# A different order for the dot products of gathered u rows, and a different pace for their fetches

## The chip, the cores and the metric

The kernel runs on one core of a Trainium2 chip. The metric is the device time of one execution in microseconds (us). Before the change three runs took 3755.72, 3756.43 and 3759.92 us; the median is 3756.43.

The engines are named as in the profile: PE is TensorE (matmuls; PEld are its weight loads), DVE is VectorE, ACT is ScalarE, POOL is GpSimd and SP is SyncE, which issues most of the plain transfers. Each engine works through its own list of instructions in order; an instruction that waits holds up all that stand behind it on its engine.

## The reference

The model is two layers of a mixer (attention, pooling, convolution, gates) with an expert feed-forward, and then two layers of a second block. Only the feed-forward of layer 0 is touched by the change:

```python
def peer_ffn(x, w_q, sub_keys, u_emb, v_emb):          # 512 tokens in layer 0, in chunks of 128
    def chunk(xc):
        q = (xc @ w_q).reshape(PEER_CHUNK, PEER_HEADS, 2, PEER_HALF)
        s = jnp.einsum('thid,hikd->thik', q, sub_keys).astype(jnp.float32)
...
        top_s, pos = lax.top_k(cand, PEER_TOPK)        # 16 experts for each of 8 heads
        eidx = jnp.take_along_axis(cidx, pos, axis=-1)
        gate = jax.nn.softmax(top_s, axis=-1)
        u = u_emb[eidx]
        hid = jax.nn.gelu(jnp.einsum('td,thkd->thk', xc, u))
        wgt = (gate * hid.astype(jnp.float32)).astype(xc.dtype)
        return jnp.einsum('thk,thkd->td', wgt, v_emb[eidx])
```

There are 16384 experts; a row of `u_emb` or `v_emb` has 1024 float32 values. A token picks 8 x 16 = 128 of them.

## The kernel before, in words

**Two ways through the feed-forward.** In layer 0 the last 128 of the 512 tokens (NROW) go the way of the reference: their 128 u rows and 128 v rows per token are gathered from memory by index. This is the class `Rows`. The other 384 tokens go the dense way: all 16384 hidden values are computed with matmuls against the whole of `u`, masked by a gate matrix, and multiplied by the whole of `v`. Each float32 matmul is made of three (high by high, high by low, low by high part), so a weight is split by ACT (`uhi`, `vhi`, L358) and DVE (`ulo`, `vlo`, L359). Layer 1 has 256 tokens, all on the dense way.

**Stages of the dense way in layer 0.** (1) `select` picks the experts. (2) `expand` turns the picks into the gate matrix: for each of 48 groups of 8 tokens DVE makes two one-hot tiles, `ohA` (L1509) and `ohB` (L1511), each from two buffers, PE multiplies them (`ps_g`, L1524 and L1525) and ACT copies the result to `stage` (L1527). Woven into (1) and (2) are the 84 hidden chunks of the first 42 blocks (`lead`, `hidden`): 24 matmuls `ps_mm` of 384 columns each (L390 to L392), then the activation `hs` (L1563). `PAY` sets how many chunks stand beside each step: a step `r` of the routing pays for 2.9 of them, a step `g` of the expansion for 0.8; what is left runs after the last `g`. (3) The value stage runs over 64 blocks in turns of two: blocks whose hidden part is still to be made (22 of them, two chunks each) and blocks whose hidden part is read back from memory (`hs_r<-hd`). A block loads 1 MB of `v` (and 1 MB of `u` if its hidden part is made here), multiplies by the gates G on DVE (L1210), splits into `Wh` and `Wl`, and PE adds it up: four products into the accumulators `keep` and two into `ps_v` (L1266), which DVE adds to `racc` (L1233). `ps_v` and `ps_mm` share three PSUM buffers. Every second block also brings 1 MB of modulation weights (`ps_mod`).

**The row path.** `Rows.ticks` is a generator; `next` on it does one tick. In its first part tick p fetches u row p of all 128 tokens (one indirect DMA on POOL, L258, 128 rows of 4 KB into a `row` tile of five buffers) and forms the dot products of row p - 3 with the tokens on DVE (L272: one custom instruction that writes its products over the row, and one that reads the sum out to `hid`). After 131 ticks the hidden values are finished and the second part does the same with v rows; there the row goes into small matmuls (`ps_row`, L304) four ticks later. It has 131 ticks too.

**When a tick happens.** After each product of PE, the program calls `spend` with the estimated time of that product. It adds the time, multiplied by `rate`, to an account, and does a tick whenever the account holds `pace` microseconds. `rate` is SLOW (0.7) from the start of the expansion until the value stage, where it is 1.0. `pace` is 3.5 in the u part and 3.25 in the v part (PACE).

```python
    def spend(self, us):
        if self.begun:
            self.due += us * self.rate
            while self.due >= self.pace:
                self.due -= self.pace
                next(self.steps, None)
```

The time of n matmuls of width w is `n * (w / 2.3 + 13) / 1000` us: 16 of 64 columns for a group of the expansion, 24 of 384 for a hidden chunk, 6 of 512 for a value product.

**What sets the order.** The program text doesn't fix the order of instructions on an engine. A planner at build time simulates all engines with estimated durations and puts each instruction on its engine's list when, by that simulation, its inputs are there. Two things bind the planner: data (with buffers), and edges written by hand. `fetch` writes one such edge: the fetch waits for `beat`, the last matmul of the last product ahead of it in the program. Its class is Sync, so the engine also waits for it on the chip by a semaphore. The dot product has no edge by hand: it follows its row's DMA and nothing else.

Of the kernel before, what the change touches and what calls it, by code (L numbers as in the profile page):

```python
# [16 lines left out]
ALU = mybir.AluOpType  # L17
# [29 lines left out]
PAY = ((2.9, 0.8), (5.0, 1.2))  # L47
NROW = 128
ROWBUFS = 5
PACE = (3.5, 3.25)  # L50
SLOW = 0.7
NPV = 4


# [154 lines left out]
class Rows:  # L209
# [21 lines left out]
    def begin(self, d1, d2, te):  # L231
# [10 lines left out]
        self.hid = pool.tile([P, P], F32, tag="hid", name="hid")  # L242
        self.steps, self.pace = self.ticks(), PACE[0]

# [11 lines left out]
    def fetch(self, name, idx):  # L256
        row = self.pool.tile([P, D], F32, tag="row", name="row", bufs=ROWBUFS)
        ins = self.nc.gpsimd.indirect_dma_start(row, None, self.p.g[name], bass.IndirectOffsetOnAxis(ap=idx, axis=0))  # L258

        self.p.tc.add_manual_dep(ins.ins, self.p.beat.ins.name, mybir.DependencyInfo(mybir.DependencyClass.Sync, mybir.DependencyReason.DATA),  # L260
                                 reason="pace")
        return row

    def ticks(self):
        nc, pool, prog = self.nc, self.pool, self.p
        rows = {}
        for p in range(P + 3):
            if p < P:
                rows[p] = self.fetch("urow", self.eu[:, p:p + 1])
            if p >= 3:  # L270
                row = rows.pop(p - 3)
                nc.vector.tensor_tensor_reduce(out=row, in0=row, in1=self.xt, op0=ALU.mult, op1=ALU.add, scale=1.0, scalar=0.0,  # L272
                                               accum_out=self.hid[:, p - 3:p - 2])
            yield
        self.pace = PACE[1]
        pt = prog.pm.tile([P, P], F32, tag="mm", name="ps_e")
        nc.tensor.transpose(pt, self.ef, prog.ident)
        self.ev = pool.tile([P, P], U32, tag="ev", name="ev")
        nc.vector.tensor_copy(self.ev, pt)
        nc.scalar.activation(self.hid, self.hid, AF.Gelu_apprx_tanh)  # L280
        nc.vector.tensor_tensor(self.hid, self.hid, self.gate, op=ALU.mult)
        order = [(r, i, g) for r in range(2) for i in range(32) for g in range(2)]
        ps = wt = None
        for n in range(P + 3):
            if n == 2:
                pt = prog.pm.tile([P, P], F32, tag="mm", name="ps_w")
                nc.tensor.transpose(pt, self.hid, prog.ident)
                wt = pool.tile([P, 2, 2, 32], F32, tag="wt", name="wt")
                nc.scalar.activation(wt.rearrange("p r g i -> p (r g i)"), pt, AF.Copy)
            if n < P:  # L290
                r, i, g = order[n]
                t = r * 64 + g * 32 + i
                rows[n] = self.fetch("vrow", self.ev[:, t:t + 1])
            if n >= 4 and n % 2 == 0:
                r, i, _ = order[n - 4]
                m = pool.tile([P, 2, 32], F32, tag="mask", name="mask2", bufs=4)
                nc.vector.tensor_tensor(m, self.hit[:, None, 31 - i:63 - i].to_broadcast([P, 2, 32]),
                                        wt[:, r, :, i:i + 1].to_broadcast([P, 2, 32]), op=ALU.mult)
                if i == 0:
                    ps = self.pv.tile([P, 512], F32, tag="rowv", name="ps_row")  # L300
                for h in range(2):
                    for g in range(2):
                        c = 32 * (2 * h + g)
                        nc.tensor.matmul(ps[c:c + 32, :], m[:, g, :], rows[n - 4 + g][:, h * 512:(h + 1) * 512],  # L304
                                         start=(i == 0), stop=(i == 31), tile_position=(0, c))
                del rows[n - 4], rows[n - 3]
                if i == 31:
                    self.add(r, ps)
            yield
# [17 lines left out]
class Prog:  # L327
# [1164 lines left out]
    def expand(self, l, T, picks, gd):  # L1492

        nc = self.nc
        with self.tc.tile_pool(name=f"expand{l}", bufs=1, reuse_waits="tile") as kp:
# [6 lines left out]
            if self.rows:  # L1502
                self.rows.begun, self.rows.rate = True, SLOW
            for n in range(T // 8 + 1):
# [421 lines left out]
```

## Time and profile before

| | before |
|---|---|
| median of 3 runs | 3756.43 us |
| profiled execution | 3769.55 us, span 3767.8 us |
| PE busy | 3588.1 us (95%) |
| DVE busy | 2460.4 us (65%) |
| ACT busy | 1635.9 us (43%) |
| POOL busy | 604.9 us (16%) |
| DMA | 777.60 MB, mean 206 GB/s |

Busy times are of the profiled execution, whose own time stands beside its span: the span runs from the first to the last instruction of the program. The expansion of layer 0 begins at about 950 us; the first u row is fetched at 976.0 us, the last at 1613.4, the first v row at 1629.3 and the last at 2153.4 us. The expansion of layer 1 ends near 2893 us.

### The profile page before, as it was taken

To read this page: it belongs to the slowest core of one execution; us is meant where nothing else is said; L and a number is where in the kernel's file an instruction comes from. 1 tells how busy PE (TensorE), PEld (TensorE's weight loads), DVE (VectorE), ACT (ScalarE), POOL (GpSimd) and SP (SyncE) were. 2 spreads that over 40 slices of the span, in tenths; PEclk is the share of its full clock that TensorE was granted. 3 is DMA by queue.
4 is the path that set the end of the run, shared out by engine and by line. 5 is a ranking of instruction groups with operands and counts; after the bars stand their busy time and mean duration, and the time that the engine had idled before them with its cause. 6 is when DMAs were issued, how large, how long until landed. Compare 5 with 4: busy or idle time off the path is not lost. (4 is left out here: it accounts for less than half of the span.)

```text
span 3767.8 us, 55009 instructions
## 1 busy us (share of the span) xinstructions
PE 3588.1 (95%) x21681; PEld 3104.3 (82%) x21681; DVE 2460.4 (65%) x4540; ACT 1635.9 (43%) x2608; POOL 604.9 (16%) x686
## 2 busy tenths in 40 slices
PE   7999999899988889899999999999999999999999
PEld 5988877789888777777766699999899888887787
DVE  5566555698687667654445576778977655556675
ACT  3333333346565322222222245455667444445454
POOL 0112222100122222222222221222000000002121
PEclk9999999999999999999999999999999999999999
DMA  5222245225687978788888823344578767666453
GB/s 208 73 90 73 79 162 190 89 90 181 237 300 277 334 268 291 287 302 299 308 287 304 286 95 119 119 153 168 188 260 291 249 238 240 235 227 221 146 177 111
DMA packets 227764, 777.60 MB, mean 206 GB/s; under 512 B 17297, under 2 KB 100753, under 8 KB 168497
## 3 DMA queue, kind: packets, MB, share of 16 engines
q1 hardware_dynamic: 165984, 567.29, 42.9%
q0 software_dynamic: 37184, 135.41, 10.4%
q10 hardware_dynamic: 24336, 71.38, 4.9%
q8 instruction: 170, 2.79, 0.3%
q14 instruction: 90, 0.73, 0.1%
HBM read 705.60 MB, written 68.42 MB: 205 GB/s over the span
## 5 line engine op out<-in xcount | busy, mean ns | idle before, releaser
L358 ACT ACTIVATE uhi<-wraw 128x1024 fp32r<-128x1024 f32 x586 | 609.7, 1057 | 868.0 <-PE ps_mm L391 341.9
L390 PE MATMUL ps_mm<-xh,uhi 128*128 128x256 f32 (+2 forms) x2952 | 960.8, 325 | 19.3 <-DVE racc L1233 9.1
L392 PE MATMUL ps_mm<-xh,ulo 128*128 128x256 f32 (+2 forms) x2952 | 945.8, 321 | 8.7 <-DVE ulo L359 8.7
L391 PE MATMUL ps_mm<-xl,uhi 128*128 128x256 f32 (+2 forms) x2952 | 944.7, 320 | 0.0
L359 DVE TENSOR_TENSOR ulo<-wraw,uhi 128x1024 fp32r<-128x1024 f32 x586 | 718.0, 1237 | 294.9 <-ACT uhi L358 274.4
L390 PEld LDWEIGHTS ps_mm<-xh,uhi 128*128 128x128 f32 x2952 | 566.2, 192 | 64.1 <-DVE racc L1233 15.8
L392 PEld LDWEIGHTS ps_mm<-xh,ulo 128*128 128x128 f32 x2952 | 565.9, 192 | 31.8 <-DVE ulo L359 10.2
L391 PEld LDWEIGHTS ps_mm<-xl,uhi 128*128 128x128 f32 x2952 | 566.4, 192 | 21.0
L358 ACT ACTIVATE vhi<-wraw 128x1024 fp32r<-128x1024 f32 x184 | 193.1, 1056 | 362.2 <-DMA wraw<-in_v 193.1
L359 DVE TENSOR_TENSOR vlo<-wraw,vhi 128x1024 fp32r<-128x1024 f32 x184 | 223.7, 1222 | 191.4 <-ACT vhi L358 190.3
L1266 PE MATMUL keep<-vhi,Wh 128*128 128x512 f32 x656 | 258.3, 394 | 2.5 <-ACT Wh L419 2.5
L258 POOL DMA_INDIRECT row<-in_urow,eu x128 | 157.4, 1230 | 638.4 <-PE ps_mm L392 472.6
L1266 PE MATMUL keep<-vlo,Wh 128*128 128x512 f32 x656 | 256.4, 391 | 2.4 <-DVE vlo L359 2.4
L1266 PE MATMUL keep<-vhi,Wl 128*128 128x512 f32 x656 | 256.5, 391 | 0.3 <-DVE Wl L420 0.3
L272 DVE CUSTOM_DVE_ANT_0 row<-row,xt 128x1024 f32<-128x1024 f32 x128 | 156.3, 1222 | 136.3 <-DMA row<-in_urow,eu 131.2
L1210 DVE TENSOR_TENSOR hs_r<-hs_r,G 128x768 f32<-128x768 f32 (+1 forms) x128 | 104.9, 822 | 175.2 <-DMA hs_r<-hd 115.3
L390 PE MATMUL ps_nar<-uhi,xh 128*128 128x256 f32 x704 | 200.7, 285 | 2.3 <-ACT cs L661 2.3
L258 POOL DMA_INDIRECT row<-in_vrow,ev x128 | 138.2, 1080 | 401.2 <-PE keep L1266 177.4
L391 PE MATMUL ps_nar<-ulo,xh 128*128 128x256 f32 x704 | 199.5, 283 | 0.8 <-DVE ulo L359 0.8
L392 PE MATMUL ps_nar<-uhi,xl 128*128 128x256 f32 x704 | 199.2, 283 | 0.0
L1527 ACT ACTIVATE stage<-ps_g 128x512 f32<-128x512 f32 x160 | 166.0, 1148 | 20.4 <-PE ps_g L1525 19.3
L1266 PE MATMUL keep<-uhi,Wh 128*128 128x512 f32 x360 | 148.3, 413 | 13.1 <-ACT uhi L358 13.1
(428 smaller groups left out, 6932.5 us busy)
## 6 DMA issues: line engine op xcount, KB each, us to landing
wraw<-in_u SPq DMA_DIRECT2D x128, 1024.0 KB
wraw<-in_v SPq DMA_DIRECT2D x128, 1024.0 KB
wraw<-in_wa SPq DMA_DIRECT2D x104, 1024.0 KB
wraw<-in_wb SPq DMA_DIRECT2D x50, 1024.0 KB
gd<-stage ACTq DMA_DIRECT2D x80, 512.0 KB
wraw_m<-in_wmod SPq DMA_DIRECT2D x24, 1024.0 KB
G<-gd SPq DMA_DIRECT2D x31, 768.0 KB
mraw<-in_wmod SPq DMA_DIRECT2D x16, 1024.0 KB
```

The costliest lines, as they stand in the source:

```text
L258: ins = self.nc.gpsimd.indirect_dma_start(row, None, self.p.g[name], bass.IndirectOffsetOnAxis(ap=idx, axis=0))
L272: nc.vector.tensor_tensor_reduce(out=row, in0=row, in1=self.xt, op0=ALU.mult, op1=ALU.add, scale=1.0, scalar=0.0, accum_out=self.hid[:, p ...
L358: nc.scalar.activation(hi, r, AF.Copy)
L359: nc.vector.tensor_tensor(lo, r, hi.bitcast(F32), op=ALU.subtract)
L390: nc.tensor.matmul(ps, lh, rh, start=(i == 0), stop=False)
L391: nc.tensor.matmul(ps, lh, rl, start=False, stop=False)
L392: self.beat = nc.tensor.matmul(ps, ll, rh, start=False, stop=(i == n - 1))
L1210: nc.vector.tensor_tensor(w, w, G.rearrange("p q j t -> p j q t"), op=ALU.mult)
L1266: self.beat = self.nc.tensor.matmul(ps, a[:, j, t], b[:, c], start=(start and j == 0 and i == 0), stop=(stop and j == 1 and i == 2), skip_ ...
L1527: nc.scalar.activation(st[:, :, tb:tb + 4].rearrange("p j t -> p t j"), pg, AF.Copy, scale=1.0 / GSCALE)
```

## The change

Two constants change: the pace (3.5 and 3.25 to 3.25 and 3.1) and the rate in the expansion (0.7 to 0.5). And the dot product gets an edge by hand to the same `beat` as the fetch of its tick. Its class is NoSync: it binds the planner's order, and no semaphore is added for it.

```diff
-PACE = (3.5, 3.25)
-SLOW = 0.7
+PACE = (3.25, 3.1)
+SLOW = 0.5
...
     def fetch(self, name, idx):
         row = self.pool.tile([P, D], F32, tag="row", name="row", bufs=ROWBUFS)
         ins = self.nc.gpsimd.indirect_dma_start(row, None, self.p.g[name], bass.IndirectOffsetOnAxis(ap=idx, axis=0))
-        self.p.tc.add_manual_dep(ins.ins, self.p.beat.ins.name, mybir.DependencyInfo(mybir.DependencyClass.Sync, mybir.DependencyReason.DATA),
-                                 reason="pace")
+        self.pace_by(ins, mybir.DependencyClass.Sync)
         return row
+
+    def pace_by(self, ins, kind):
+
+        self.p.tc.add_manual_dep(ins.ins, self.p.beat.ins.name, mybir.DependencyInfo(kind, mybir.DependencyReason.DATA), reason="pace")
...
             if p >= 3:
                 row = rows.pop(p - 3)
-                nc.vector.tensor_tensor_reduce(out=row, in0=row, in1=self.xt, op0=ALU.mult, op1=ALU.add, scale=1.0, scalar=0.0,
-                                               accum_out=self.hid[:, p - 3:p - 2])
+                ins = nc.vector.tensor_tensor_reduce(out=row, in0=row, in1=self.xt, op0=ALU.mult, op1=ALU.add, scale=1.0, scalar=0.0,
+                                                     accum_out=self.hid[:, p - 3:p - 2])
+                self.pace_by(ins, mybir.DependencyClass.NoSync)
```

## Rows read from the trace of the kernel before

**Rows 1.** The page, part 2: busy tenths in 40 slices of the span.

```profile
PE   7999999899988889899999999999999999999999
```

**Rows 2.** Windows: busy (count) of PE, PEld, DVE, ACT, POOL; granted clock; DMA share, GB/s.

```profile
976.00:1294.00 318.00, 284.40 (x2019) 271.73 (x2017) 234.73 (x258) 174.24 (x205) 70.55 (x59) 0.95 0.82 298
1294.00:1625.00 331.00, 289.25 (x1319) 239.61 (x1320) 220.43 (x298) 86.06 (x102) 88.66 (x73) 0.93 0.80 285
1625.00:2165.00 540.00, 522.52 (x2569) 367.03 (x2562) 254.94 (x343) 141.85 (x165) 138.22 (x128) 0.98 0.85 299
2760.00:2900.00 140.00, 139.81 (x1417) 138.37 (x1416) 113.08 (x97) 110.64 (x138) 1.65 (x3) 1.00 0.79 278
```

**Rows 3.** Waits of PE in 976:1294, then 1294:1625: total us, times, longest.

```profile
PE ps_g L1524 <- DVE ohB L1511: 25.7, 9, 4.2
...
PE ps_mm L392 <- DVE ulo L359: 1.6, 1, 1.6
...
PE ps_mm L390 <- DVE racc L1233: 25.4, 8, 6.3
PE keep L1266 <- ACT uhi L358: 9.5, 3, 4.1
...
PE keep L1266 <- DVE ulo L359: 1.2, 2, 0.8
```

**Rows 4.** Waits of DVE in 976:1294 (first two), then 1294:1625.

```profile
DVE row L272 <- DMA row<-in_urow,eu: 63.3, 22, 6.5
...
DVE row L272 <- issue: 4.8, 1, 4.8
...
DVE row L272 <- DMA row<-in_urow,eu: 67.9, 29, 6.8
```

**Rows 5.** Timeline of POOL, then DVE, near 1199 and 1220 us: start, length, [idle before].

```profile
1199.61 1.43 POOL L258 DMA_INDIRECT row<-in_urow,eu  x1 [11.47 <-PE ps_mm L392]
...
1215.09 1.85 POOL L258 DMA_INDIRECT row<-in_urow,eu  x1 [4.22 <-PE ps_mm L392]
1220.55 1.07 POOL L258 DMA_INDIRECT row<-in_urow,eu  x1 [2.00 <-PE ps_mm L392]
...
1210.23 1.22 DVE L272 CUSTOM_DVE_ANT_0 row<-row,xt 128x1024 f32<-128x1024 f32 x1 [6.46 <-DMA row<-in_urow,eu]
...
1211.38 1.22 DVE L1509 TENSOR_TENSOR ohA<-io,picks 128x2048 f16<-128x2048 f16 x1
...
1232.24 1.23 DVE L272 CUSTOM_DVE_ANT_0 row<-row,xt 128x1024 f32<-128x1024 f32 x1 [4.47 <-DMA row<-in_urow,eu]
```

**Rows 6.** Waits of DVE in 2760:2900 (expansion of layer 1).

```profile
DVE ohA L1509 <- PE ps_g L1525: 14.2, 12, 1.9
```

**Rows 7.** Timeline of PE at a wait in the value stage.

```profile
1319.24 0.69 PE L390 MATMUL ps_mm<-xh,vhi 128*128 128x384 f32 x1 [3.34 <-DVE racc L1233]
```

**Rows 8.** Windows of 4 us just behind that wait, columns as in rows 2.

```profile
1319.00:1323.00 4.00, 3.76 (x12) 3.76 (x13) 4.00 (x5) 0.88 (x1) 0.00 (x0) 0.50 0.57 238
1324.00:1328.00 4.00, 4.00 (x25) 4.00 (x24) 1.23 (x1) 1.44 (x2) 1.79 (x2) 1.00 0.72 252
```

**Rows 9.** Line L272 in 976:1294: ns min/median/max, first and last start.

```profile
L272 DVE CUSTOM_DVE_ANT_0 row<-row,xt x54: 1210/1223/1308, 980.6 to 1292.7; 128x1024 f32<-128x1024 f32 x54
L272 DVE DVE_READ_ACCUMULATOR2_ANT hid<- x54: 75/81/85, 981.7 to 1293.9; 128x1 f32 x54
```

**Rows 10.** Windows with the highest DMA rates in the band, columns as in rows 2.

```profile
1200.00:1300.00 100.00, 94.10 (x533) 88.66 (x530) 57.06 (x72) 39.18 (x50) 27.06 (x25) 0.97 0.89 327
1220.00:1270.00 50.00, 44.37 (x242) 43.73 (x241) 25.08 (x31) 16.05 (x22) 11.44 (x11) 0.93 0.97 364
```

**Rows 11.** Groups of PE in 1625:2165: count | busy us, mean ns | idle before.

```profile
L304 PE MATMUL ps_row<-row,mask 128*32 128x512 f32 x512 | 72.2, 619 | 0.0
```

**Rows 12.** Waits of POOL in 1294:1625.

```profile
POOL row L258 <- DVE hid L272: 22.8, 7, 9.2
```

## The prediction

> **What bounds the kernel now.** The page comes first: TensorE (PE) is busy 95% of the span, and in the 40 slices (94 us each) its digit falls below 9 only at the start, once near 700 us, and in a band from 1036 to 1600 us [rows 1]. Work outside that band can't be what a change of the row path moves, so the second view is the windows. From 976 us (first u-row fetch) to 1294 us, the expansion, PE is busy 284.40 of 318 us at a mean granted clock of 0.95. From 1294 to 1625 us, where the value blocks run beside the rest of the u rows, it is busy 289.25 of 331 us at 0.93. From 1625 to 2165 us (v rows) it is 522.52 of 540 at 0.98. The expansion of layer 1, which has the same one-hot work and no rows, is busy 139.81 of 140 us at 1.00 [rows 2]. So rows cost PE 33.6 + 41.8 us of idle time in the two u stretches, and a lower clock beside it.
>
> Who ends PE's idle time is the third view. In the expansion it is `ohB` on VectorE (DVE), 25.7 us, and DVE's `ulo`, 1.6. In the second stretch it is DVE for 32.1 us in five rows, of which `racc` with 25.4 is the first and `ulo` with 1.2 the last, and ScalarE's weight copy for 9.5 [rows 3]. DVE itself waits for one thing above all: the dot product of a u row (L272) for the row's DMA, 63.3 + 4.8 us and 67.9 us [rows 4]. The timeline shows how. The row fetched at 1199.61 is waited for from 1203.77, and the next `ohA` and `ohB` stand behind that wait until 1211.38. The fetch that follows it by three ticks, which in the program stands just ahead of this dot product, starts only at 1215.09 [rows 5]. The planner has thus put the dot product some 11 us ahead of its place in the program. In layer 1, DVE waits for PE at `ohA` (14.2 us) and not PE for DVE [rows 6]. The chain is: row DMA, DVE, PE.
>
> A stall costs more than its length. After a 3.34 us wait [rows 7] the granted clock is 0.50 (1.2 GHz) over 4 us, with 12 matmuls of 384 columns in them; soon after it is 1.00 (2.4 GHz), with 25 [rows 8]. That restart alone lost some 2 us on top.
>
> **Part by part: counts.** `spend` gives 0.653 us of program time for a group of 8 tokens, 4.319 for a hidden chunk, 1.414 for a value product (from its formula). The expansion has 48 groups and 57 of the 84 leading hidden chunks (27 are paid for before it, nine `r` steps of 2.9): 31.4 + 246.2 = 277.5 program us. At 3.5/0.7 = 5.0 us a tick that is 55 ticks, and 54 dot products stand in that stretch of the trace [rows 9]. After: 3.25/0.5 = 6.5 us a tick, 42 ticks. The value stage has 724.4 program us. Its u part goes from 264.7 (76 ticks at 3.5, less the remainder) to 287.4 (89 at 3.25), its v part from 425.8 to 405.9. Both end before 724.4 (at 690 and 693), so nothing is pushed to the flush.
>
> **Expansion.** The new edge makes the planner place the dot product after the tensor product that ends the tick three fetches later, about 3 x 6.5 x 318/277.5 = 22 us after its own fetch. The longest lag that I find in this stretch between a fetch and a dot product that waited for it is 1232.24 - 1220.55 = 11.7 us [rows 5], so the 68.1 us of DVE stall go, and 13 dot products of 1.223 + 0.081 us move out. No wait instruction is added, since the edge is an order and not a semaphore. What can be late next on DVE is its own load (234.7 of 318 us, 74%), less than the 81% at which layer 1 kept PE full [rows 2]. Gone: 27.3 us of idle, and of the clock loss (0.05 x 318 = 15.9 us) the same share, 12.9. Taken: -40 us. Ends: 0 if the edge changes no order, -49.5 if all idle and clock loss go.
>
> **Value stage, u part.** If all idle and clock loss went (41.8 + 0.07 x 331 = 65 us), PE would need 266 us for 264.7 program us, so 289 us for 287.4. Here the cover may fail, because the transfers grow. The stretch moved 285 GB/s [rows 2], 94.3 MB; a `row` tile is 128 x 4096 bytes = 0.524 MB, so 73 rows are 38.3 MB and the rest 56.1 MB. After: 89 rows (46.7) and 56.1 x 287.4/264.7 = 60.9, together 107.6 MB. In 289 us that is 372 GB/s. The trace has 364 GB/s over 50 us at a share of 0.97, 327 over 100 us [rows 10] and 299 over the 540 us of the v rows [rows 2]. I take 320, near the 100 us row, so 336 us. Ends: 289 us (nothing but PE) and 360 us (today's pace, which is also what 299 GB/s gives).
>
> The page "DMA: Bandwidth & Descriptors" of the Trainium skill (Specifications) puts the HBM limit of one core at about 358 GB/s; by it the u part would take 301 us, an estimate, and not 336. No stretch of 100 us here holds that rate, so the rows decide.
>
> **Value stage, v part.** 540 us hold 72.2 us of row matmuls [rows 11]; the other 467.8 us go with program time: 467.8 x 405.9/425.8 + 72.2 = 518 us. Its transfers are 94.3 x 405.9/425.8 + 67.1 (128 rows) = 157 MB, 303 GB/s, as today. So u and v parts together go from 871 to 336 + 518 = 854 us: -17. Ends: -64 and +7.
>
> Fetches themselves move only in time; POOL is busy 88.66 of 331 us [rows 2] and serves little else. But POOL is also where a late dot product would return: seven fetches waited 22.8 us for a dot product to free one of the five row buffers [rows 12].
>
> **Sum.** -40 - 17 = -57 us, to be taken from the profiled execution (3769.55 us around a span of 3767.8), 13.1 us above the median of 3756.43. As a difference it is carried over whole: 3756.4 - 57 = 3699 us. The likeliest case's own range is 3676 to 3725 (u part at 299 to 345 GB/s, clock share given back or not).
>
> **Rivals.**
> A. The forecast: stalls go, the u part then leans on the transfers. For it: DVE waits for one DMA, and PE for DVE. Chance 0.55, 3699 us.
> B. Transfers keep up and PE is the only bound: -40 - 64 = -104, 3652 us. For it: 364 GB/s occurs. Against: DMA share is already 0.80 to 0.85 with PE idling. Chance 0.13. The limit in the Trainium skill ("DMA: Bandwidth & Descriptors", Specifications) would give 301 us for the u part and 3664 us in all, an estimate.
> C. The edge doesn't do what it says (an order between two engines that the planner drops or meets anyway). Then only pacing is left. In the expansion 13 dot products fewer at 1.30 + 68.1/54 = 2.56 us are 33 us of DVE time, at 33.6/68.1 = 0.49 us of PE idle per us of stall: -16. The u part stays at 331/264.7 = 1.25 per program us: 359.5 + 518 - 871 = +6.5. Together -10, 3746 us. Against: the fetch's own edge to the same product holds, as its releasers show [rows 5]. Chance 0.22.
> D. Slower: the ring of five row buffers becomes the bound. The dot product now stands behind everything DVE does for that tick, its buffer comes free late, the fetch two ticks later starts late, and its own dot product waits again, now each of 89 and not 29 of 74. At 67.9/29 = 2.34 us each and 41.8/67.9 = 0.62 us of PE per us of stall the u part is 289 + 129 = 418 us: +65, less 40, so 3781 us. It is slower than before from a u part of 393 us on, which is 1.9 us of wait per dot product. For it: three ticks there are only some 11 us, as long as the longest lags, and [rows 12]. Against: today's 29 waits there already hold such lags, with the dot products ahead of their place, and came to 2.34 us each; behind it each should be shorter. Chance 0.10.
>
> **Chances and range.** About 0.2% (7.5 us) is what can be told from no change. A, B and most of C (0.13) are faster by more: 0.81. C's rest (0.07) and a little of D are the same: 0.08. D and C's far end are slower: 0.11. The range takes A whole, half of B and most of C: 3660 to 3752.
>
> **What would show it.** Right: DVE's wait for `row<-in_urow` under 15 us in the expansion, PE's wait for `ohB` nearly gone and clock 0.99 there; 41 or 42 dot products in it; u part at 310 GB/s or more with a DMA share near 0.9, and ScalarE's wait for weights as PE's largest. C: each dot product still starts before the fetch three ticks on. D: POOL's wait for `hid` over 100 us. The prediction is wrong if the expansion still idles by 20 us, or if PE idles as long with DVE no longer waiting for rows.

## The result and the profile after

The changed kernel takes 3702.45 us (four runs, 3693.91 to 3707.05) against 3758.18 us before on the same chip: a ratio of 0.9849, 95% interval 0.983 to 0.9869, so it is 1.5% faster. The forecast was 3699 us.

The profiled execution has a span of 3699.7 us, 68.1 less than the one shown before. That one stood above its own median; a second profile of the kernel before (an experiment below) has a span of 3758.1 us, and the stretches are compared with it. They are cut at events of the program: the first u fetch, the first fetch behind the ticks of the expansion, the first v fetch, the last v fetch.

| stretch, us | before, second profile | after | difference |
|---|---|---|---|
| to the first u fetch | 974.6 | 975.9 | +1.3 |
| expansion (55 ticks; after 42) | 316.0 | 269.2 | -46.8 |
| u part of the value stage (76 ticks; after 89) | 335.8 | 341.7 | +5.9 |
| v part | 519.9 | 492.8 | -27.1 |
| rest | 1611.7 | 1620.2 | +8.5 |

These cuts follow the ticks and not the work, and the change moves the ticks: the expansion's stretch of before holds 44 matmuls of the value stage (`keep` and `ps_v`), that of after holds 8. A second cut therefore goes by PE's own work, and has the same hidden and value matmuls in every version: from the first one-hot product (`ps_g`) to the first `keep`, from there to the last `keep` of layer 0, and from there to the end. By work the expansion goes from 306.7 to 273.0 us, the value stage from 888.1 to 857.8, and what follows from 1594.4 to 1598.7.

The windows of the stretches of the table, first of the second profile of before, then of after (columns as in [rows 2], which were cut at nearly the same events):

```profile
974.60:1290.60 316.00, 282.83 (x2015) 269.84 (x2013) 234.00 (x256) 174.09 (x205) 71.59 (x59) 0.96 0.84 301
1290.60:1626.40 335.80, 297.71 (x1343) 246.19 (x1342) 224.93 (x305) 87.04 (x103) 88.71 (x73) 0.92 0.79 281
1626.40:2146.30 519.90, 505.28 (x2486) 358.17 (x2486) 246.66 (x331) 137.43 (x160) 138.86 (x127) 0.98 0.86 305
```

```profile
975.90:1245.00 269.10, 263.67 (x1979) 255.23 (x1977) 215.83 (x224) 169.63 (x201) 52.62 (x45) 0.99 0.89 322
1245.00:1586.70 341.70, 314.30 (x1462) 261.68 (x1462) 250.27 (x343) 95.24 (x113) 108.68 (x86) 0.96 0.86 312
1586.70:2079.50 492.80, 483.62 (x2385) 337.25 (x2384) 237.98 (x323) 132.11 (x155) 135.13 (x128) 0.99 0.88 313
```

In the expansion PE now idles 5.4 us and its clock is 0.99. In the u part it still idles 27.4 us at 0.96. The waits of PE, of after, first in the expansion and then in the u part, answer to [rows 3]:

```profile
PE ps_g L1527 <- ACT stage L1530: 3.1, 7, 0.5
PE ps_mm L393 <- ACT hs L1566: 2.2, 1, 2.2
...
PE ps_mm L393 <- DVE racc L1236: 16.1, 6, 4.5
PE ps_mm L393 <- ACT uhi L361: 7.3, 2, 4.2
PE keep L1269 <- ACT uhi L361: 2.2, 1, 2.2
```

`ohB` is gone from them. DVE's waits of after, in the expansion (first two) and in the u part, answer to [rows 4]:

```profile
DVE ulo L362 <- ACT uhi L361: 22.2, 9, 6.3
DVE ohA L1512 <- PE ps_g L1528: 17.0, 21, 2.7
...
DVE ulo L362 <- ACT uhi L361: 57.7, 15, 6.8
DVE hs_r L1213 <- DMA hs_r<-hd: 14.1, 5, 4.1
DVE vlo L362 <- ACT vhi L361: 10.1, 5, 3.2
DVE row L274 <- DMA row<-in_urow,eu: 4.5, 3, 2.4
```

The 136 us that DVE waited for rows (133 in the second profile) are 4.5 us, and in the expansion it waits for PE at `ohA`, as layer 1 did in [rows 6]. The timeline of after, POOL and then DVE, shows one dot product in its new place (compare [rows 5]):

```profile
1103.62 0.94 POOL L258 DMA_INDIRECT row<-in_urow,eu  x1 [9.85 <-PE ps_mm L395]
...
1120.43 1.31 POOL L258 DMA_INDIRECT row<-in_urow,eu  x1 [5.52 <-PE ps_mm L395]
...
1119.71 1.22 DVE L274 CUSTOM_DVE_ANT_0 row<-row,xt 128x1024 f32<-128x1024 f32 x1
```

The row fetched at 1103.62 is used at 1119.71, 16 us later and without a wait, just as the fetch three ticks on begins.

### The profile page after: what moved, and what is told of

Read it like the earlier page. It is cut to its first block, busy times and chain, and to the rows that moved or that the text cites. A ratio compares the mean times of both kernels' runs of the same rounds, so it can differ in the third digit from the quotient of the medians.

```text
span 3699.7 us, 55016 instructions
## 1 busy us (share of the span) xinstructions
PE 3574.0 (97%) x21681; PEld 3097.0 (84%) x21681; DVE 2461.5 (67%) x4540; ACT 1634.3 (44%) x2608; POOL 604.0 (16%) x686
## 4 chain that ended last, share of the span: by engine, by line
PE 41%; DVE 4%; DMA 2%; ACT 1%; issue 1%; POOL 1%; DVEq 0%; ACTq 0%; SPq 0%; POOLq 0%
PE keep L1269 12%; PE ps_mm L393 5%; PE ps_mm L395 5%; PE ps_mm L394 5%; PE ps_wide L395 2%; PE ps_wide L393 2%; PE ps_wide L394 2%; PE ps_v L1269 1%; DVE ulo L362 1%; PE ps_nar L393 1%; PE ps_nar L395 1%; PE ps_nar L394 1%; DMA wraw<-in_v 1%; PE ps_mm L414 1%; PE ps_row L307 1%
## 5 line engine op out<-in xcount | busy, mean ns | idle before, releaser
L1269 PEld LDWEIGHTS keep<-vhi,Wh 128*128 128x128 f32 x656 | 123.7, 189 | 36.8 <-issue 9.2
```

What stands on the lines that cost most here:

```text
L1269: self.beat = self.nc.tensor.matmul(ps, a[:, j, t], b[:, c], start=(start and j == 0 and i == 0), stop=(stop and j == 1 and i == 2), skip_ ...
```

## The experiments

Times are medians; ratios are against the kernel before on the same chip, with 95% intervals. Stretches by ticks are those of the table above; stretches by work are the expansion, the value stage and what follows, as cut there (the kernel after: 273.0, 857.8, 1598.7).

| kernel | us | ratio | by ticks: expansion, u, v, rest (us) | by work: expansion, value stage, rest (us) |
|---|---|---|---|---|
| edge alone | 3706.3 | 0.985 [0.9825, 0.9875] | 279.1, 321.4, 511.3, 1617.0 | 274.7, 860.1, 1599.6 |
| pace alone | 3763.5 | 1.0007 [0.9993, 1.0021] | 300.7, 382.1, 491.7, 1618.0 | 303.9, 897.8, 1596.5 |
| edge and pace, rate 0.7 | 3706.1 | 0.9839 [0.9812, 0.9866] | 290.2, 282.2, 499.8, 1664.4 | 283.0, 859.4, 1595.6 |
| edge in the expansion only | 3735.4 | 0.9942 [0.9917, 0.9967] | 271.0, 376.5, 491.6, 1618.9 | 274.1, 892.1, 1597.3 |
| edge in the value stage only | 3728.1 | 0.9923 [0.9899, 0.9948] | 299.9, 337.6, 492.9, 1617.0 | 303.7, 853.9, 1595.4 |
| four row buffers | 3695.5 | 0.9838 [0.981, 0.9866] | 271.1, 338.0, 488.2, 1619.2 | 274.9, 849.5, 1597.6 |
| no modulation loads | 3649.9 | 0.9715 [0.9691, 0.9739] | 273.2, 301.7, 478.6, 1617.3 | 277.0, 803.7, 1595.7 |
| a quarter of their bytes | 3691.1 | 0.982 [0.9803, 0.9836] | 272.1, 334.2, 490.9, 1617.7 | 275.9, 848.5, 1596.1 |
| modulation moved | 3771.7 | 1.004 [1.0026, 1.0055] | 269.8, 309.8, 477.8, 1737.0 | 273.7, 810.9, 1715.5 |
| rows spread | 3692.5 | 0.9826 [0.981, 0.9842] | 275.5, 333.3, 517.2, 1591.1 | 273.9, 843.4, 1605.5 |
| own modulation buffer | 3697.7 | 0.9825 [0.9811, 0.9838] | 271.6, 333.2, 498.1, 1616.5 | 275.4, 854.7, 1594.9 |

**The two halves of the change.** Theory 1: the stalled dot products were the cost and the order removes them. Theory 2: the thinner fetches in the expansion give the gain.

The edge alone, on the changed kernel:

```diff
-PACE = (3.25, 3.1)
-SLOW = 0.5
+PACE = (3.5, 3.25)
+SLOW = 0.7
```

> The order edge without the new pace (3.5 and 3.25 us, rate 0.7 as before). Theory 1 (the stalled dot products were the cost, and the order removes them): DVE's wait for rows falls from 136 us to under 15 us, PE no longer waits for ohB, and the time falls by 35 to 60 us against before; DVE carries 13 more dot products in the expansion than with the new pace (17 us of DVE time at 76% load), so the expansion may keep a few us of PE idle. Theory 2 (the gain comes from thinning the fetches in the expansion): within 10 us of before.

The pace alone:

```diff
-                self.pace_by(ins, mybir.DependencyClass.NoSync)
```

> The new pace (3.25 and 3.1 us, rate 0.5) without the order edge. Theory 1: dot products still start ahead of the fetch three ticks on, DVE still waits about 1.2 us for each on average (130 us or more in all), and the time is 0 to 15 us under before (rival C of the prediction: -10). Theory 2: 45 to 60 us under before.

The edge with the expansion's rate back:

```diff
-SLOW = 0.5
+SLOW = 0.7
```

> The changed kernel with the rate in the expansion back at 0.7 (4.64 us a tick, about 60 ticks there, 71 left for the value stage). Theory 1 with a u part that leans on the transfers: expansion loses little (DVE 13 to 18 dot products more, about 20 us of DVE time in a stretch with slack), the u part of the value stage is 16 rows shorter, so the total is within 10 us of the changed kernel, either side. Theory 2: most of the gain is lost, 35 us or more above the changed kernel.

And the kernel before once more, unchanged, for a second profile:

> The kernel before, a second profile of it. The two profiled executions differ by 68 us while the medians differ by 56. If the first profile of before was 10 us long by chance, the second has a span near 3745 to 3757 us and shows which stretch differs; if the profile itself adds to this kernel, it is near 3768 again.

The second profile of before came out at 3759.89 us with a span of 3758.1, a little above the range that was expected if the first was long by chance, and 10 us below it. The other runs of this kernel beside it go from 3750 to 3772 us, so both profiles lie within its spread; the stretches above are taken from the second, which is nearer the median.

The edge alone has the whole gain, the pace alone none. With the edge alone DVE waits 1.5 us for rows in all. With the pace alone it waits for rows as long as ever: 69.0 + 77.6 us, against 67.2 + 65.8 in the second profile of before. In the expansion that is on fewer dot products: 18 of 40 waited, against 21 of 54. The waits of PE and DVE in the expansion and of DVE in the u part with the pace alone, and then DVE's in the expansion of the second profile of before:

```profile
PE ps_g L1526 <- DVE ohB L1513: 22.3, 9, 3.9
...
DVE row L274 <- DMA row<-in_urow,eu: 69.0, 18, 8.4
...
DVE row L274 <- DMA row<-in_urow,eu: 77.6, 34, 6.0
...
DVE row L273 <- DMA row<-in_urow,eu: 67.2, 21, 8.2
```

By ticks the pace alone seems to save 15 us in the expansion, but most of that is value work that falls behind the earlier cut. By work it saves 2.8 us there, the value stage takes 9.7 us more, and the median is 1 us above that of before, where 0 to 15 below it was expected. With the edge in place the pace does little: by work 274.7 to 273.0 us in the expansion and 860.1 to 857.8 in the value stage, and the medians of edge alone and of the whole change lie 4 us apart, inside both intervals. So a gain of the new pace isn't shown. Rate 0.7 costs 10 us in the expansion and 1.6 in the value stage by work; the median is 4 us higher, within the 10 us that theory 1 expected and again inside the intervals.

**Where the edge acts.** The edge is written only while the rate is that of the expansion, or only while it is 1.0:

```diff
-                self.pace_by(ins, mybir.DependencyClass.NoSync)
+                if self.rate < 1.0:
+                    self.pace_by(ins, mybir.DependencyClass.NoSync)
```

> The changed kernel with the order edge only on the dot products that the program forms in the expansion (42 ticks); in the value stage they are placed freely, as before. If both stretches gain by the edge as the sum of stretches says (expansion alone 300.7 to 269 us, value part 382 + 492 to 342 + 493 us), this keeps the 30 us of the expansion and loses the 40 us of the value stage: 3730 to 3745 us. If the value part doesn't need the edge (its stalls would be hidden by the transfers anyway): within 10 us of the changed kernel.

```diff
-                self.pace_by(ins, mybir.DependencyClass.NoSync)
+                if self.rate == 1.0:
+                    self.pace_by(ins, mybir.DependencyClass.NoSync)
```

> The counterpart: the edge only on the dot products of the value stage. By the sum of stretches the 40 us there stay gained and the expansion idles again by about 25 us: 3725 to 3740 us, with PE waiting some 22 us for ohB. If the edge in the expansion alone carries the gain: 3755 us or more.

Both medians lie where they were expected if both stretches gain. Against the pace alone the first takes 30 us off the expansion and 6 off the value stage by work, the second 44 us off the value stage and nothing off the expansion. Each stretch gains by its own edges; together the gains are 80 us, where the whole change has 71 in these two stretches.

**The ring of row buffers (rival D).**

```diff
-ROWBUFS = 5
+ROWBUFS = 4
```

> The changed kernel with four row buffers instead of five (rival D's mechanism brought on): a fetch now needs the buffer of the dot product that the order puts one tick ahead of it, not two. If the ring is near its limit: POOL waits for hid over 100 us (18 us with five), DVE waits for rows again by 50 us or more, and the time rises by 20 to 65 us. If it has room: POOL's wait for hid rises below 60 us, DVE's wait for rows stays below 20 us, and the time is within 8 us of the changed kernel.

The ring has room, as the second case of the expectation has it. With four buffers POOL waits for dot products in the u part for 50.3 us (13.3 with five), and DVE still waits only 3.2 us for rows. The waits of POOL, then of DVE:

```profile
POOL row L258 <- DVE hid L274: 50.3, 19, 8.7
...
DVE row L274 <- DMA row<-in_urow,eu: 3.2, 2, 1.9
```

The time is not above that of five buffers. A late fetch cost nothing here, because its row still landed before its dot product's place.

**What holds the u part now.** The forecast had it leaning on the bytes that the queues can move. First the 24 modulation loads of the value stage are left out; the same matmuls read another tile, so layer 1's modulation is not computed:

```diff
-                    raw = self.raw("wraw_m")
-                    nc.sync.dma_start(raw, src)
+                    raw = self.rows.xt
...
+                    d = c % 2 if raws is None and not pool else c
```

> The changed kernel without the 24 loads of 1 MB of modulation weights in the value stage; the same matmuls read a tile that is already there, so the modulation values are not the reference's. In the u part this takes out about 11 of 107 MB, 10%. If the u part is now bound by the transfers (the forecast's step): it falls from 342 us to 305 to 320 us at about the same 312 GB/s, PE waits less for ulo, uhi and racc, and the total falls by 20 to 40 us. If transfers don't set its pace: u part within 8 us of 342, GB/s falls to about 280, total within 10 us. Two raw weight buffers are also used less, which helps in the same direction.

The u part falls to 301.7 us, of which PE is busy 300.53, at 317 GB/s: a little below the 305 to 320 us that a bound by the transfers was to give, and now PE is nearly full. But that run frees more than bytes. The modulation loads also take turns in the three raw weight buffers, and places in the list of SP, where their issue waits for a buffer ahead of the weight loads (44.2 us at L624 in the u part of after). So the second run cuts the bytes and keeps the turns and the places. All four matmuls of a step read the first 512 columns, so layer 1's modulation is again not computed:

```diff
-                    nc.sync.dma_start(raw, src)
+                    nc.sync.dma_start(raw[:, :512], src[:, :512])
...
+                    d = 0 if raws is None and not pool else c
```

> The changed kernel with each of the 24 modulation loads of the value stage cut to its first 512 of 2048 columns, which all four matmuls then read: three quarters of their bytes go (8 of 107 MB in the u part), the weight buffers are taken in turn exactly as before. If it is the bytes that hold the u part (the run without these loads also freed buffers): three quarters of that run's gain or more, so 3655 to 3672 us, u part 305 to 318 us. If it is the buffers: within 12 us of the changed kernel, 3690 us or more.

The bytes go and the time hardly follows: 334.2 us at 293 GB/s, where an unchanged 312 GB/s would have given about 314. By work the value stage is 9.3 us shorter than that of after; four row buffers, which move the same bytes, were 8.3 us shorter, so it isn't shown that fewer bytes gain anything. The windows of the u part of the two runs:

```profile
1247.60:1549.30 301.70, 300.53 (x1462) 250.90 (x1461) 252.93 (x346) 97.22 (x116) 106.94 (x86) 1.00 0.90 317
```

```profile
1247.80:1582.00 334.20, 310.38 (x1457) 258.87 (x1456) 250.08 (x343) 95.52 (x114) 106.33 (x87) 0.96 0.83 293
```

What stays with the quarter of the bytes is the wait for weights. The waits of ACT in its u part, and those of the queue of SP, which issues the loads:

```profile
ACT uhi L361 <- DMA wraw<-in_v: 95.2, 13, 12.6
...
SPq L351 <- DVE vlo L362: 65.7, 11, 11.7
...
SPq L351 <- DMA wraw<-in_v: 56.6, 13, 10.1
SPq L351 <- DVE ulo L362: 56.2, 14, 5.8
SPq L624 <- DVE ulo L362: 25.2, 7, 5.6
SPq L351 <- PE ps_mod L627: 19.4, 4, 6.7
```

The issue of a weight load (L351) waits for DVE (121.9 us) or the modulation matmul (19.4) to give a raw buffer back, or for an earlier load to land (56.6). The load is then on its way for a median of 7.0 us to landing, and ACT, DVE and PE stand behind it. That points to the turn-round of the buffers, and not to the rate; it is read from the waits, and no run here shows it by itself.

Two versions tried to use this with every value computed. One moves 16 of the 24 loads to the mixer of layer 1, through one half-size buffer:

```diff
-                mods = self.modulation(0, [1, 2], pool=mp, bufs=1) if l == 0 else iter(())
+                mods = self.modulation(l, [1, 2], pool=mp, bufs=1)
...
-                mods = self.modulation(1, range(3)) if l == 0 else iter(())
+                mods = self.modulation(1, [0]) if l == 0 else iter(())
...
-                    if n % 2 == 0 and n > 1:
+                    if n % 7 == 0 and n > 1:
```

> The changed kernel with two thirds of layer 1's modulation (16 of the 24 MB) made in layer 1's mixer, beside its pooling, where the trace shows about 120 GB/s, instead of in the value stage of layer 0; the last 8 MB are spread over all 64 blocks there (4 to 5 of them in the u part instead of 11). All values are computed. If transfers hold the value stage of layer 0: 25 to 45 us under the changed kernel, 3660 to 3680 us, less what the mixer of layer 1 loses to loads through one half-size buffer. If they don't: no change, or up to 20 us more for those waits in the mixer.

The value stage gained a little more than was expected (by work 810.9 us against 857.8), and the mixer of layer 1 lost more than twice that: the rest is 117 us longer, where up to 20 had been put down, and the total is a miss. Each half load landed 3.0 to 5.7 us after its issue, and with one buffer the matmuls of a step wait for it in PE's list. PE's waits in 2100:2800 of that run:

```profile
PE ps_mod L635 <- DMA mraw<-in_wmod: 63.0, 23, 5.0
```

Two windows of 75 us in that stretch show PE busy for 47.65 and 44.35 us at a clock of 0.73 and 0.75, so the clock goes down beside the waits.

The other leaves the loads in the value stage and gives them a buffer of their own, paid for by the fifth row buffer:

```diff
-ROWBUFS = 5
+ROWBUFS = 4
...
-                    raw = self.raw("wraw_m")
-                    nc.sync.dma_start(raw, src)
...
+                        raw = half = self.rows.pool.tile([P, 1024], F32, tag="modh", name="modh", bufs=1)
+                        nc.sync.dma_start(half, src[:, c * 512:c * 512 + 1024])
```

> The changed kernel with four row buffers (that alone gave 3695 us); the 4 KB saved hold a buffer of its own for the modulation weights, which come in halves of 512 KB, one per block instead of 1 MB every second block. Every value is computed, all bytes are still moved, and the three raw buffers serve the u and v weights alone. If those buffers hold the value stage (as the run without the loads against the run with a quarter of their bytes says): u part 300 to 320 us at 330 GB/s or more, ScalarE's wait for wraw<-in_v (93 us) under 40 us, total 3650 to 3675 us. If the bytes hold it after all: u part 335 us or more, total 3685 us or more.

The waits went as expected and the time did not: the total, 3697.7 us, falls where the expectation put the case that the bytes hold the stretch. ACT no longer waits for weights, and PE neither for `racc` nor for `uhi`; all that PE waits for in the u part is the new buffer. The window of the u part and PE's waits in it:

```profile
1248.30:1581.50 333.20, 317.79 (x1462) 254.61 (x1461) 252.99 (x346) 97.15 (x116) 99.62 (x86) 0.98 0.90 322
...
PE ps_mod L632 <- DMA modh<-in_wmod: 15.4, 9, 3.1
```

The single half buffer is filled too late (its loads land a median of 7.1 us after issue), so a new wait took the old one's place. PE's busy time is also 17 us above that of the run without the loads. 13 us of these are in the modulation matmuls themselves. Their group in the u part, first with the own buffer, then without the loads:

```profile
L632 PE MATMUL ps_mod<-modh,sc 128*32 128x512 f32 x88 | 24.7, 641 | 15.4 <-DMA modh<-in_wmod 15.4
...
L626 PE MATMUL ps_mod<-xt,sc 128*32 128x512 f32 x88 | 11.7, 605 | 0.0
```

So this run can't tell buffers from bytes: it frees the three raw buffers and puts a wait of its own into PE's list.

**Spreading the rows.**

```diff
-PACE = (3.25, 3.1)
-SLOW = 0.5
+PACE = (3.45, 3.3)
+SLOW = 0.6
```

> The changed kernel with the rows spread evenly to the end of the value stage: rate 0.6, pace 3.45 and 3.3 us (48 ticks in the expansion, the last tick at 719 of 724 program us). The bytes stay the same and get some 26 program us more. If transfers hold the stretch: 5 to 15 us under the changed kernel. If the rows' own order was all: within 5 us of it. If the last v rows come too late for the end of the stage: above it.

This is 3692.5 us, 10 under the changed kernel's median and in the range expected if transfers weigh on the stretch; the intervals of the two overlap, so the gain isn't shown. By the ratios to before, this version, four row buffers and the own modulation buffer can't be told apart.

## Why the prediction was right, and where it was not

- **The chain row DMA, DVE, PE: right.** The edge alone removes the row waits and 1.5% of the time, the pace alone removes neither, and each stretch gains where its edges are. Rival C needed the edge to do nothing. In the expansion a dot product now starts a mean of 0.3 us ahead of the fetch three ticks on; in the second profile of before it started 7.7 us ahead of it.
- **Expansion: -40 forecast; -46.8 measured by ticks, -38.8 on the same work.** The stretch of before ends at its 44th value matmul; after has that one 8.0 us behind its own cut, so 8 of the 46.8 us are a shift of the cut. PE's idle time fell by 27.7 us, as forecast (27.3). Its busy time fell by 19.2; without the 8 us of the 36 value matmuls that is 11, where 12.9 were put down for the clock. The signs named beforehand for this stretch came out, but for 39 dot products in the stretch instead of 41 or 42.
- **u and v parts: -17 forecast, -21.2 measured, by a step whose reason was half wrong.** On the same work, from the 44th value matmul to the last `keep`, it is -25.2 (873.2 to 848.0 us). The u part was put at 336 us, from 331, and took 341.7, from 335.8. The forecast's v part ran on to 2165 us and so was put at 518, from 540; by fetches it took 492.8, from 519.9. But "I take 320" GB/s as a limit of the transfers is not what holds the u part. The edge-alone run moved 340 GB/s over the 279 us of its expansion, above the 327 of [rows 10], and a cut of the bytes with the buffers kept let the rate fall to 293 and the time by 7.5 us only. So 320 came near the time without being the limit: that is partly luck. The waits point to raw weight buffers that come round too late, which is argued and not shown. ScalarE does wait for weights, as forecast (97.1 us for `wraw<-in_v`). But PE's largest wait was forecast to be for ScalarE, and it is for `racc` on DVE with 16.1 us, behind `ulo`, which waits for ScalarE's `uhi`. The highest rate of a whole stretch here, 340 GB/s, is below the 358 GB/s of the Trainium skill ("DMA: Bandwidth & Descriptors", Specifications), and no run here shows that figure as the bound; [rows 10] has 364 over 50 us, a little above it.
- **v part: -22 forecast by program time alone, -27.1 measured.** PE idles 9.2 us there instead of 14.6, and the clock is 0.99 instead of 0.98.
- **The rest: unchanged by the forecast, 8.5 us longer by ticks.** About half of that, 4.1 us, is value work that now stands behind the last v fetch: the last `keep` comes 21.5 us after it, and came 17.4 us after it before. What follows that `keep` is 4.3 us longer, within the 1594 to 1600 us that all versions show but two, which move other work there.
- **Rival C's prices** can be checked on the pace alone, and by work they fail in both stretches: -16 priced and -2.8 measured in the expansion, +6.5 priced and +9.7 measured in the value stage. The price let the row waits go down with the number of dot products; in the expansion they stayed at 69.0 us. In the u part each dot product waited as long as before (0.87 us of DVE's time on average), but PE idled 56.0 us there instead of 38.1.
- **The restart of the clock** was read one wait too late. The granted clock was at 0.50 by 1315 us, before the 3.34 us wait of [rows 7] and behind a longer one. The 2 us that were put down for the restart belong to both waits together. The matmul behind the longer wait, and a window from there on (columns as in [rows 2]):

```profile
1315.11 0.80 PE L1266 MATMUL keep<-uhi,Wh 128*128 128x512 f32 x1 [4.13 <-ACT uhi L358]
...
1315.00:1323.20 8.20, 4.75 (x13) 4.25 (x14) 8.11 (x10) 3.00 (x4) 0.00 (x0) 0.50 0.43 145
```

- **Rival D fell**: one buffer less did not bring it on.
- **What stays open** is how much of the 40 us that the u part gave without modulation loads is buffers and how much bytes. Fewer bytes alone gave 7.5 us (9.3 in the value stage by work, where four row buffers gave 8.3); buffers alone, with the bytes kept, moved the wait and gave 5 in the u part against the run with four row buffers, but lost 10 in the v part. Leaving the loads out gave 40. That run also took their places out of SP's list, where loads behind them wait, and no run tests that by itself.

## What to carry to other kernels

When an in-order engine waits for a transfer, look at where the program has the instruction and where the planner has put it: an instruction placed ahead of the data that it needs stalls all that stands behind it, and here an order without a semaphore was enough to put it back. Price a stall on PE with the clock after it, not by its length. Before calling a stretch bound by transfers, cut the bytes and keep the buffers: if the rate falls instead of the time, the rate wasn't the limit, and the waits say where to look next. And when a change moves the events that a stretch is cut at, compare the stretches on the same work.

## What the runs showed that was not expected

- Thinner fetches made each wait longer: in the expansion 18 waits took 69.0 us with the pace alone, 21 took 67.2 us before. Why isn't shown.
- A mix of 1 MB loads and gathered rows ran at 340 GB/s for 279 us at a DMA share of 0.93, with PE busy 270.31 us of them at a clock of 1.00:

```profile
976.60:1255.60 279.00, 270.31 (x2015) 260.40 (x2013) 234.29 (x255) 172.79 (x205) 69.53 (x58) 1.00 0.93 340
```
